# Attention's value matmuls over four token tiles at a time instead of two, in a hybrid encoder layer on one Trainium2 core

## The chip, the cores and the metric

The kernel runs on one NeuronCore of a Trainium2 chip. The metric is the device time of one execution in microseconds (us): the median of several runs. The engines are PE (TensorE; its weight loads are shown apart, as PEld), DVE (VectorE), ACT (ScalarE), POOL (GpSimd) and SP, which issues most DMAs.

## What is computed

One layer: a half-step feed-forward network, a mixer, a second feed-forward network, a final norm. The mixer has two groups of heads side by side, latent attention and retention, and one output projection over both. The change lies in attention alone, which has 8 heads of width 64 over 1024 tokens and no mask:

```python
def block(args):
    qn, qp = args
    s = (jnp.einsum('bqhd,bkhd->bhqk', qn, k_nope).astype(jnp.float32)
         + jnp.einsum('bqhr,bkr->bhqk', qp, k_pe).astype(jnp.float32))
    p = jax.nn.softmax(s * MLA_SCALE, axis=-1)
    return jnp.einsum('bhqk,bkhd->bqhd', p.astype(v.dtype), v)
```

## The kernel before, in words

All matmuls are in float32r. To keep float32's accuracy an operand is split in two by `split` (line 71): ACT casts the source to the upper part (line 75), DVE subtracts that from the source for the lower part (line 79). A product of two split operands is three matmuls (`mm3`, lines 115 to 120).

`attention` (line 1440) walks over 64 steps, 8 heads by 8 tiles of 128 queries. I count the tiles through all heads, 0 to 63. For one tile:

- `scores` (line 1481): six matmuls of 512 columns into a PSUM tile `mm` of 128 x 1024, of which there are two. DVE finds the row's extreme (`mx`, line 1490), ACT takes the exponential into `pr` (line 1494; two buffers) and its row sums.
- `flip` (line 1498): eight PE transposes (line 1507) turn `pr` over, four into each of two PSUM tiles `tp`; ACT's cast and DVE's subtraction bring them as split halves into `pT`, which holds two query tiles, 256 columns, and has two buffers.
- `values` (line 1513), once for two tiles: for each of 8 key tiles and each half of the split one matmul (line 1520), the values as weights and 256 columns of `pT` streaming, 16 in all into one PSUM tile `dn`. ACT copies the result out (`ota`, line 1523).
- `finish` (line 1526): two PE transposes (line 1530) back to token rows, a DVE reduction that adds the two halves (line 1532), a reciprocal of the sums (line 1535) and POOL's multiplication by it into `mixed` (line 1536), which is the queries' memory `qn`, free by then.

`queries` (line 1467) prepares a head's queries by eight transposes (line 1474); `keys` and `keys2` prepare the keys of two heads. The loop at the end gives the order in which steps are handed on: scores of step i, flip of i-1, values of i-2 and finish of i-4:

```python
            if 0 <= i - 1 < len(seq):
                flip(*seq[i - 1])
            for lag, fn in ((2, values), (4, finish)):
                if 0 <= i - lag < len(seq) and seq[i - lag][1] % 2 == 1:
                    fn(seq[i - lag][0], seq[i - lag][1] // 2)
```

A scheduler then lays the instructions of each engine out in a fixed order before the run; so an engine's instructions can stand between others than the code suggests, but on the chip each engine keeps its order, and waits by semaphores. After attention the generator `out_project` (line 1563) goes on with the output projection, whose first transposes (line 1602) and weights already stand among the last tiles.

Of the kernel before, what the change touches and what calls it, by code (L numbers as in the profile page):

```python
# [12 lines left out]
F32 = mybir.dt.float32  # L13
F32R = mybir.dt.float32r
# [3 lines left out]
ALU = mybir.AluOpType  # L18
# [3 lines left out]
P = 128  # L22
S = 1024
NT = S // P
# [4 lines left out]
HA, HR, HD = 8, 8, 64  # L29
# [32 lines left out]
class Layer:  # L62
# [1377 lines left out]
    def attention(self, small, pool, after):  # L1440
# [35 lines left out]
                hs = slice(half * 512, (half + 1) * 512)  # L1476
                self.split(ps[0:QH], qT[0:QH, 0, hs], qT[0:QH, 1, hs])

        sums, pts = {}, {}

        def scores(h, t):
            kT, qT = self.kT[h % 2], qTs[h]
            ts_ = slice(t * P, (t + 1) * P)
            ps = self.ps.tile([P, S], F32, name="mm")
            for n in range(2):
                ns = slice(n * 512, (n + 1) * 512)
                self.mm3(ps[:, ns], (qT[0:QH, 0, ts_], qT[0:QH, 1, ts_]),
                         (kT[0:QH, 0, ns], kT[0:QH, 1, ns]), True, True)
            mx = small.tile([P, 1], F32, name="mx", bufs=4)
            v.tensor_reduce(out=mx, in_=ps, axis=AX.X, op=ALU.min)  # L1490
            pr = pool.tile([P, S], F32, name="pr")
            if t % 2 == 0:
                sums[h, t // 2] = small.tile([P, 2], F32, name="sum", bufs=6)
            nc.scalar.activation(out=pr, in_=ps, func=AF.Exp, scale=-1.0, bias=mx,
                                 accum_out=sums[h, t // 2][:, t % 2:t % 2 + 1])
            pts[h, t] = pr

        def flip(h, t):
            pr = pts.pop((h, t))
            if t % 2 == 0:  # L1500
                pts[h, "T", t // 2] = pool.tile([P, 2, NT, 2 * P], F32R, name="pT")
            pT = pts[h, "T", t // 2]
            for half in range(2):
                ps = self.ps.tile([P, 512], F32, name="tp")
                for j in range(4):
                    kt = half * 4 + j
                    nc.tensor.transpose(ps[:, j * P:(j + 1) * P], pr[:, kt * P:(kt + 1) * P],  # L1507
                                        self.ident)
                k4, qs = slice(half * 4, half * 4 + 4), slice(t % 2 * P, (t % 2 + 1) * P)
                self.split(ps.rearrange("p (j q) -> p j q", j=4), pT[:, 0, k4, qs],  # L1510
                           pT[:, 1, k4, qs])

        def values(h, u):
            pT = pts.pop((h, "T", u))
            ps = self.ps.tile([P, 512], F32, name="dn")
            o = ps[:, 0:2 * P]
            for kt in range(NT):
                vl = self.vhl[:, kt, h].rearrange("p s d -> p (s d)")
                for x in range(2):
                    nc.tensor.matmul(o, vl, pT[:, x, kt], start=(kt == 0 and x == 0),  # L1520
                                     stop=(kt == NT - 1 and x == 1))
            ot = small.tile([P, 2 * P], F32, name="ota")
            nc.scalar.copy(out=ot, in_=o)
            pts[h, "O", u] = ot

        def finish(h, u):
            ot = pts.pop((h, "O", u))
            ps = self.ps.tile([P, 512], F32, name="dn")
            for j in range(2):
                nc.tensor.transpose(ps[:, j * P:(j + 1) * P], ot[:, j * P:(j + 1) * P], self.ident)  # L1530
            on = small.tile([P, 2, HD], F32, name="ona", bufs=1)
            v.tensor_reduce(out=on, in_=ps[:, 0:2 * P].rearrange("p (j s e) -> p j e s", j=2, s=2),
                            axis=AX.X, op=ALU.add)
            ri = small.tile([P, 2], F32, name="ri", bufs=6)
            v.reciprocal(out=ri, in_=sums.pop((h, u)))
            nc.gpsimd.tensor_tensor(out=mixed[:, 2 * u:2 * u + 2, h // 2, h % 2 * HD:(h % 2 + 1) * HD], in0=on,
                                    in1=ri.unsqueeze(2).broadcast_to([P, 2, HD]), op=ALU.mult)

        seq = [(h, t) for h in range(HA) for t in range(NT)]
        for i in range(len(seq) + 6):  # L1540
            if i < len(seq):
                h, t = seq[i]
                if t == 0 and h == 0:
                    queries(0, (0,))
                    keys(0)
                    queries(0, (1,))
                scores(h, t)
                if t == 1 and h + 1 < HA:
                    queries(h + 1)
                if t == 3:  # L1550
                    if h % 2 == 0:
                        keys2(h // 2)
                    elif h + 1 < HA:
                        keys(h // 2 + 1)
            if 0 <= i - 1 < len(seq):
                flip(*seq[i - 1])
            for lag, fn in ((2, values), (4, finish)):
                if 0 <= i - lag < len(seq) and seq[i - lag][1] % 2 == 1:
                    fn(seq[i - lag][0], seq[i - lag][1] // 2)
            if i - len(seq) in (-6, -5, -4, -3, 0):  # L1560
                next(after)

# [127 lines left out]
```

## Time and profile before

| | us |
|---|---|
| median of 3 runs | 2043.13 |
| lowest, highest | 2036.83, 2044.27 |
| the profiled execution | 2037.01 |
| its span, first to last instruction | 2035.3 |

| engine | busy us | share of the span |
|---|---|---|
| PE | 1974.2 | 97% |
| PE weight loads | 1697.3 | 83% |
| DVE | 1312.0 | 64% |
| ACT | 816.0 | 40% |
| POOL | 689.4 | 34% |

The numbers of the profile come from one execution; the profiled execution's own time is its span and some 1.7 us around it. Times in views count from the span's start. A matmul's row shows its pipelined length, longer than the distance to the next matmul's start; what a matmul takes from PE's queue is that distance. "idle before <-" says how long an engine stood and which instruction ended it. Attention lies between 1035 and 1270 us.

### The profile page before, as it was taken

The page shows a single profiled execution, that of the slowest core. Times are in us where ns is not written, and L with a number is a line of the kernel's source. Part 1 is how long each engine was busy: PE and PEld are TensorE (multiplying, and loading weights), DVE is VectorE, ACT ScalarE, POOL GpSimd, SP SyncE. Part 2 cuts the span into 40 slices and gives each one's busy share as a digit, 9 for nine tenths or more (in the row PEclk, how much of TensorE's full clock was granted, in tenths as well). Part 3 has the DMA queues.
Part 4 walks back from the last instruction along what each step waited for, and adds up shares of the span by engine and source line. Part 5 has one row for each costly group of instructions (what it writes and reads, how often), then busy time and mean ns, then how long its engine had stood idle before and what let it go on. Part 6 is the DMA issues. An engine that isn't in the chain of part 4 may idle for free.

```text
span 2035.3 us, 28607 instructions
## 1 busy us (share of the span) xinstructions
PE 1974.2 (97%) x10776; PEld 1697.3 (83%) x10776; DVE 1312.0 (64%) x2032; ACT 816.0 (40%) x1422; POOL 689.4 (34%) x614
## 2 busy tenths in 40 slices
PE   6999999999999999999999999999999999999998
PEld 4778888877778899998788888997788888878876
DVE  7766566676656545427878887448565665666566
ACT  5322222233444322236567776234223223234444
POOL 0256656673310013213521110000465665672012
PEclk9999999999999999999999999999999999999999
DMA  5244453468766011200100000141354444478773
GB/s 176 61 162 134 171 175 132 173 199 273 264 217 207 28 53 43 53 22 1 58 1 1 1 1 22 42 156 48 104 176 166 152 158 166 154 254 317 227 228 113
DMA packets 209338, 258.86 MB, mean 127 GB/s; under 512 B 14128, under 2 KB 126000, under 8 KB 209200
## 3 DMA queue, kind: packets, MB, share of 16 engines
q1 hardware_dynamic: 208048, 254.93, 37.8%
q8 instruction: 85, 1.39, 0.3%
q10 hardware_dynamic: 1152, 2.10, 0.3%
q14 instruction: 53, 0.43, 0.1%
HBM read 185.15 MB, written 71.83 MB: 126 GB/s over the span
## 4 chain that ended last, share of the span: by engine, by line
PE 40%; DVE 3%; DMA 3%; ACT 2%; issue 1%; POOL 1%; SPq 0%; ACTq 0%; DVEq 0%; POOLq 0%
PE mm L290 11%; PE dn L290 6%; PE dn L1520 3%; PE tp L290 3%; PE tp L1507 3%; PE mm L624 2%; DMA rawd<-wdt 2%; PE dn L118 2%; PE dn L120 2%; PE dn L119 2%; PE mm L118 1%; PE mm L120 1%; PE mm L119 1%; DVE wd L79 1%; PE dn L624 1%; PE tp L624 1%
## 5 line engine op out<-in xcount | busy, mean ns | idle before, releaser
L290 PE MATMUL mm<-xt,gu 128*128 128x512 f32 x1584 | 382.8, 390 | 0.4 <-ACT xt L75 0.3
L290 PEld LDWEIGHTS mm<-xt,gu 128*128 128x128 f32 x1584 | 296.5, 188 | 62.4 <-issue 1.0
L79 DVE TENSOR_TENSOR wd<-rawd,wd 128x1024 fp32r<-128x1024 f32 x143 | 194.9, 1368 | 126.1 <-ACT wd L75 125.9
L79 DVE TENSOR_TENSOR gu<-s,gu 128x512 fp32r<-128x512 f32 x176 | 180.8, 1028 | 139.6 <-ACT gu L75 139.6
L290 PE MATMUL dn<-x,gu 128*128 128x512 f32 x1056 | 258.8, 393 | 1.3 <-ACT x L75 1.3
L290 PEld LDWEIGHTS dn<-x,gu 128*128 128x128 f32 x1056 | 197.7, 189 | 42.8 <-ACT x L75 2.0
L75 ACT CAST wd<-rawd 128x1024 fp32r<-128x1024 f32 x143 | 150.2, 1052 | 193.0 <-DMA rawd<-wdt 59.6
L270 POOL TENSOR_TENSOR s<-raw 128x512 f32<-128x512 f32 x40 | 55.4, 1386 | 396.6 <-DMA raw<-in_ffn_w_up 198.2
L624 PE MATMUL mm<-wd 128*128 128x512 f32 x792 | 182.6, 390 | 2.1 <-DVE wd L79 2.1
L624 PEld LDWEIGHTS mm<-wd 128*128 128x128 f32 x792 | 148.1, 188 | 35.7 <-DVE wd L79 4.4
L79 DVE TENSOR_TENSOR gu<-raw,gu 128x512 fp32r<-128x512 f32 x132 | 123.1, 933 | 69.7 <-ACT gu L75 69.6
L322 DVE TENSOR_TENSOR h<-mm,h 128x512 f32<-128x512 f32 x176 | 120.8, 686 | 70.7 <-PE mm L290 70.3
L352 ACT ACTIVATE h<-h 128x512 f32<-128x512 f32 x44 | 27.8, 632 | 291.4 <-DVE h L322 291.4
L624 PE MATMUL dn<-wd 128*128 128x512 f32 x462 | 133.3, 392 | 8.5 <-DVE wd L79 8.5
L290 PE MATMUL tp<-xt,gu 128*128 128x512 f32 x528 | 128.0, 390 | 4.8 <-ACT gu L75 2.5
L624 PE MATMUL tp<-wd 128*128 128x512 f32 x462 | 130.2, 389 | 0.0
L75 ACT CAST gu<-s 128x512 fp32r<-128x512 f32 x176 | 104.2, 618 | 63.7 <-POOL s L271 59.6
L290 PE MATMUL mm<-x,gu 128*128 128x512 f32 x528 | 127.1, 390 | 0.0
L290 PEld LDWEIGHTS tp<-xt,gu 128*128 128x128 f32 x528 | 98.6, 188 | 27.3 <-ACT gu L75 3.4
L290 PEld LDWEIGHTS mm<-x,gu 128*128 128x128 f32 x528 | 99.0, 188 | 21.1 <-DVE h L322 0.6
L624 PEld LDWEIGHTS dn<-wd 128*128 128x128 f32 x462 | 85.8, 188 | 30.7 <-DVE wd L79 13.3
L633 POOL TENSOR_TENSOR h<-h,u 128x512 f32<-128x512 f32 x24 | 45.0, 1907 | 177.7 <-DMA rawd<-hid 89.2
(356 smaller groups left out, 3917.3 us busy)
## 6 DMA issues: line engine op xcount, KB each, us to landing
hid<-h SPq DMA_DIRECT2D x154, 256.0 KB, 3.2
rawd<-hid SPq DMA_DIRECT2D x154, 256.0 KB, 3.2
raw<-in_ffn_w_gate SPq DMA_DIRECT2D x52, 512.0 KB, 3.9
raw<-in_ffn_w_up SPq DMA_DIRECT2D x44, 512.0 KB, 4.1
rawd<-wdt SPq DMA_DIRECT2D x88, 256.0 KB, 3.7
early<-in_ffn_w_down SPq DMA_DIRECT2D x40, 512.0 KB, 5.6
wdt<-early SPq DMA_DIRECT2D x80, 256.0 KB, 4.5
rawd<-in_ffn_w_down SPq DMA_DIRECT2D x66, 256.0 KB, 3.4
```

Source lines behind the costliest of these rows:

```text
L75: a = nc.scalar.copy(out=hi, in_=src)
L79: b = eng.tensor_tensor(out=lo, in0=src, in1=hi.bitcast(F32), op=ALU.subtract)
L118: mm(out, l[0], r[0], start=start, stop=False)
L119: mm(out, l[0], r[1], start=False, stop=False)
L120: mm(out, l[1], r[0], start=False, stop=stop)
L270: tt(out=s[1], in0=u[:, h1], in1=u[:, h2], op=ALU.add)
L290: nc.tensor.matmul(out, l[:, p], r[:, q], start=start and dt == 0 and i == 0, stop=dt == 3 and i == 2, skip_group_check=True)
L322: v.tensor_tensor(out=out, in0=ps, in1=other, op=ALU.add)
L624: nc.tensor.matmul(out, w[:, p, 0, ts_], w[:, q, 1], start=start and i == 0, stop=stop and i == 2, skip_group_check=True)
L633: nc.gpsimd.tensor_tensor(out=q, in0=q, in1=u[:, t], op=ALU.add)
L1507: nc.tensor.transpose(ps[:, j * P:(j + 1) * P], pr[:, kt * P:(kt + 1) * P], self.ident)
L1520: nc.tensor.matmul(o, vl, pT[:, x, kt], start=(kt == 0 and x == 0), stop=(kt == NT - 1 and x == 1))
```

## The change

Values and finish now work on four tiles. `G = 4` takes the place of the 2 in the sums, in `values` and in `finish`, so that a value matmul has 512 columns and there are 8 x 2 blocks of 16. `pT` becomes two tiles, `pT0` and `pT1`, each with the four key tiles of one half, both parts of the split and 512 query columns. Each has one buffer, 32 KB a partition together, as the two buffers of `pT` before. A group's first flip can write `pT0` once the values of the group before have read it; so values and finish are handed on before the flip of the same step. `ota` has one buffer of 512 columns, the reduction writes straight into `mixed`, and POOL multiplies there in place.

```diff
-        sums, pts = {}, {}
+        sums, pts, G = {}, {}, 4
...
-            if t % 2 == 0:
-                pts[h, "T", t // 2] = pool.tile([P, 2, NT, 2 * P], F32R, name="pT")
-            pT = pts[h, "T", t // 2]
+            if t % G == 0:
+                pts[h, "T", t // G] = [pool.tile([P, 2, NT // 2, G * P], F32R, name=f"pT{half}",
+                                                 bufs=1) for half in range(2)]
...
-                k4, qs = slice(half * 4, half * 4 + 4), slice(t % 2 * P, (t % 2 + 1) * P)
-                self.split(ps.rearrange("p (j q) -> p j q", j=4), pT[:, 0, k4, qs],
-                           pT[:, 1, k4, qs])
+                pT, qs = pts[h, "T", t // G][half], slice(t % G * P, (t % G + 1) * P)
+                self.split(ps.rearrange("p (j q) -> p j q", j=4), pT[:, 0, :, qs], pT[:, 1, :, qs])
...
-            ps = self.ps.tile([P, 512], F32, name="dn")
-            o = ps[:, 0:2 * P]
+            o = self.ps.tile([P, 512], F32, name="dn")
...
-                    nc.tensor.matmul(o, vl, pT[:, x, kt], start=(kt == 0 and x == 0),
+                    nc.tensor.matmul(o, vl, pT[kt // 4][:, x, kt % 4], start=(kt == 0 and x == 0),
                                      stop=(kt == NT - 1 and x == 1))
-            ot = small.tile([P, 2 * P], F32, name="ota")
+            ot = small.tile([P, G * P], F32, name="ota", bufs=1)
...
-            for j in range(2):
+            for j in range(G):
                 nc.tensor.transpose(ps[:, j * P:(j + 1) * P], ot[:, j * P:(j + 1) * P], self.ident)
-            on = small.tile([P, 2, HD], F32, name="ona", bufs=1)
-            v.tensor_reduce(out=on, in_=ps[:, 0:2 * P].rearrange("p (j s e) -> p j e s", j=2, s=2),
+            on = mixed[:, G * u:G * (u + 1), h // 2, h % 2 * HD:(h % 2 + 1) * HD]
+            v.tensor_reduce(out=on, in_=ps.rearrange("p (j s e) -> p j e s", j=G, s=2),
                             axis=AX.X, op=ALU.add)
...
+            for lag, fn in ((2, values), (4, finish)):
+                if 0 <= i - lag < len(seq) and seq[i - lag][1] % G == G - 1:
+                    fn(seq[i - lag][0], seq[i - lag][1] // G)
             if 0 <= i - 1 < len(seq):
                 flip(*seq[i - 1])
-            for lag, fn in ((2, values), (4, finish)):
-                if 0 <= i - lag < len(seq) and seq[i - lag][1] % 2 == 1:
-                    fn(seq[i - lag][0], seq[i - lag][1] // 2)
```

How the scheduler laid it out. On PE before, in head 0 around the flip of tile 6 (L1507 is a flip's transposes, L1520 the values, L1530 the finish, L118 to L120 the scores):

```order
L1520 MATMUL dn<-pT,vhl 128x256 x4
L1507 MATMUL tp<-ident,pr 128x128 x8
L1520 MATMUL dn<-pT,vhl 128x256 x12
L1530 MATMUL dn<-ident,ota 128x128 x2
L118 MATMUL mm<-kT_8929,qTa 128x512
```

Values stand on both sides of the flip. On PE after, at the end of the first group of four, with the flips of tiles 4 and 5 (now L1509) and the scores between:

```order
L1520 MATMUL dn<-pT_9276,vhl 128x512 x8
L1520 MATMUL dn<-pT_9277,vhl 128x512 x8
L1509 MATMUL tp<-ident,pr 128x128 x8
L118 MATMUL mm<-kT_8929,qTa 128x512
L119 MATMUL mm<-kT_8929,qTa 128x512
L120 MATMUL mm<-kT_8929,qTa 128x512
L118 MATMUL mm<-kT_8929,qTa 128x512
L119 MATMUL mm<-kT_8929,qTa 128x512
L120 MATMUL mm<-kT_8929,qTa 128x512
L1509 MATMUL tp<-ident,pr 128x128 x8
```

All sixteen values stand in a row, and only scores stand between flips of a group. On ACT before, in head 2 (a pair of casts is one flip, ACTIVATE pr the exponential):

```order
L1523 COPY ota<-dn 128x256
L75 CAST pT<-tp 128x4x128 x2
L1494 ACTIVATE pr,sum<-mm,mx 128x1024
L75 CAST pT<-tp 128x4x128 x2
L1494 ACTIVATE pr,sum<-mm,mx 128x1024
L1523 COPY ota<-dn 128x256
```

On ACT after, in head 2 for the group of tiles 20 to 23:

```order
L1523 COPY ota<-dn 128x512
L75 CAST pT_9975<-tp 128x4x128
L75 CAST pT_9976<-tp 128x4x128
L75 CAST pT_9975<-tp 128x4x128
L75 CAST pT_9976<-tp 128x4x128
L1496 ACTIVATE pr,sum<-mm,mx 128x1024
L75 CAST pT_9975<-tp 128x4x128
L75 CAST pT_9976<-tp 128x4x128
L1496 ACTIVATE pr,sum<-mm,mx 128x1024
L75 CAST pT_9975<-tp 128x4x128
L75 CAST pT_9976<-tp 128x4x128
L1496 ACTIVATE pr,sum<-mm,mx 128x1024
```

The casts of the group's first two flips come one behind the other, then exponentials (now L1496) and casts by turns. Over all 64 flips, 27 now stand in two halves with scores or values between them, 10 before.

## Rows read from the trace of the kernel before

**Rows 1.** The page, part 1: busy time, share and instructions of each engine

```profile
PE 1974.2 (97%) x10776; PEld 1697.3 (83%) x10776; DVE 1312.0 (64%) x2032; ACT 816.0 (40%) x1422; POOL 689.4 (34%) x614
```

**Rows 2.** View of windows, attention: PE, PEld, DVE, ACT, POOL busy; clock; DMA

```profile
1100.00:1160.00 60.00, 59.86 (x407) 53.37 (x406) 49.01 (x74) 43.46 (x86) 6.12 (x11) 1.00 0.00 1
```

**Rows 3.** Grouped lines, attention 1035 to 1270 us: busy, mean ns, idle before

```profile
L79 DVE TENSOR_TENSOR pT<-tp,pT 128x512 fp32r<-128x512 f32 x128 | 83.1, 684 | 14.9 <-ACT pT L75 14.9
L1490 DVE TENSOR_REDUCE mx<-mm 128x1 f32<-128x1024 f32 x64 | 78.0, 1220 | 18.2 <-PE mm L120 18.2
```

**Rows 4.** Timeline of PE, four tiles of head 2: start, length, line

```profile
1101.25 1.04 PE L1507 MATMUL tp<-ident,pr 128*128 128x128 f32 x8
1102.05 0.48 PE L118 MATMUL mm<-kT,qTa 96*128 96x512 f32 x1
1102.37 0.39 PE L119 MATMUL mm<-kT,qTa 96*128 96x512 f32 x1
...
1103.50 0.64 PE L1520 MATMUL dn<-pT,vhl 128*128 128x256 f32 x4
1104.12 1.09 PE L1507 MATMUL tp<-ident,pr 128*128 128x128 f32 x8
1104.97 1.69 PE L1520 MATMUL dn<-pT,vhl 128*128 128x256 f32 x12
1106.49 0.38 PE L1530 MATMUL dn<-ident,ota 128*128 128x128 f32 x2
1106.63 0.48 PE L118 MATMUL mm<-kT,qTa 96*128 96x512 f32 x1
...
1108.11 1.04 PE L1507 MATMUL tp<-ident,pr 128*128 128x128 f32 x8
...
1114.95 1.04 PE L1507 MATMUL tp<-ident,pr 128*128 128x128 f32 x8
```

**Rows 5.** Timeline of ACT and PE's weight loads, the same stretch

```profile
1101.89 1.07 ACT L75 CAST pT<-tp 128x512 fp32r<-128x512 f32 x2 [1.53 <-PE tp L1507]
...
1102.85 1.13 ACT L1494 ACTIVATE pr<-mm,mx 128x1024 f32<-128x1024 f32 x1
...
1104.12 0.86 PEld L1507 LDWEIGHTS tp<-ident,pr 128*128 128x128 f32 x8 [0.18 <-ACT pr L1494]
...
1104.82 1.08 ACT L75 CAST pT<-tp 128x512 fp32r<-128x512 f32 x2 [0.75 <-PE tp L1507]
```

**Rows 6.** Grouped lines, retention stage 905 to 1010 us

```profile
L1197 DVE TENSOR_REDUCE rq<-tp 128x256 f32<-128x512 f32 x16 | 10.9, 681 | 0.0
```

**Rows 7.** Timeline of PE, the first tiles of attention

```profile
1043.69 1.46 PE L1507 MATMUL tp<-ident,pr 128*128 128x128 f32 x8
...
1046.14 0.88 PE L1520 MATMUL dn<-pT,vhl 128*128 128x256 f32 x6
1046.98 1.09 PE L1507 MATMUL tp<-ident,pr 128*128 128x128 f32 x8
...
1053.38 1.09 PE L1507 MATMUL tp<-ident,pr 128*128 128x128 f32 x8
```

**Rows 8.** Timeline of ACT, the same place

```profile
1045.71 1.13 ACT L1494 ACTIVATE pr<-mm,mx 128x1024 f32<-128x1024 f32 x1
```

**Rows 9.** Timeline of PE, the last group: first flip of four

```profile
1253.72 1.09 PE L1507 MATMUL tp<-ident,pr 128*128 128x128 f32 x8
```

**Rows 10.** Timeline of PE, where the output projection begins

```profile
1269.57 0.36 PE L118 MATMUL dn<-ckvT,kT 128*128 128x256 f32 x1
```

**Rows 11.** View of windows: a wait, the stretch behind it, two others

```profile
915.00:920.00 5.00, 2.47 (x21) 2.26 (x19) 3.73 (x5) 3.01 (x6) 1.31 (x2) 1.00 0.00 0
920.00:925.00 5.00, 4.12 (x23) 4.15 (x24) 4.49 (x8) 4.93 (x12) 0.00 (x0) 0.67 0.00 0
1000.00:1030.00 30.00, 27.49 (x158) 23.57 (x159) 27.94 (x65) 16.68 (x30) 16.67 (x23) 1.00 0.16 54
1040.00:1046.00 6.00, 6.00 (x28) 5.10 (x29) 3.31 (x6) 3.22 (x7) 0.30 (x1) 0.72 0.01 3
```

More of the change, by code (lines that the diff above doesn't have):

```diff
@@ L1491, in scores @@
             pr = pool.tile([P, S], F32, name="pr")
-            if t % 2 == 0:
-                sums[h, t // 2] = small.tile([P, 2], F32, name="sum", bufs=6)
+            if t % G == 0:
+                sums[h, t // G] = small.tile([P, G], F32, name="sum", bufs=6)
             nc.scalar.activation(out=pr, in_=ps, func=AF.Exp, scale=-1.0, bias=mx,
-                                 accum_out=sums[h, t // 2][:, t % 2:t % 2 + 1])
+                                 accum_out=sums[h, t // G][:, t % G:t % G + 1])
             pts[h, t] = pr
@@ L1499, in flip @@
             pr = pts.pop((h, t))
-            if t % 2 == 0:
-                pts[h, "T", t // 2] = pool.tile([P, 2, NT, 2 * P], F32R, name="pT")
-            pT = pts[h, "T", t // 2]
+            if t % G == 0:
+                pts[h, "T", t // G] = [pool.tile([P, 2, NT // 2, G * P], F32R, name=f"pT{half}",
+                                                 bufs=1) for half in range(2)]
             for half in range(2):
@@ L1528, in finish @@
             ps = self.ps.tile([P, 512], F32, name="dn")
-            for j in range(2):
+            for j in range(G):
                 nc.tensor.transpose(ps[:, j * P:(j + 1) * P], ot[:, j * P:(j + 1) * P], self.ident)
-            on = small.tile([P, 2, HD], F32, name="ona", bufs=1)
-            v.tensor_reduce(out=on, in_=ps[:, 0:2 * P].rearrange("p (j s e) -> p j e s", j=2, s=2),
+            on = mixed[:, G * u:G * (u + 1), h // 2, h % 2 * HD:(h % 2 + 1) * HD]
+            v.tensor_reduce(out=on, in_=ps.rearrange("p (j s e) -> p j e s", j=G, s=2),
                             axis=AX.X, op=ALU.add)
-            ri = small.tile([P, 2], F32, name="ri", bufs=6)
+            ri = small.tile([P, G], F32, name="ri", bufs=6)
             v.reciprocal(out=ri, in_=sums.pop((h, u)))
-            nc.gpsimd.tensor_tensor(out=mixed[:, 2 * u:2 * u + 2, h // 2, h % 2 * HD:(h % 2 + 1) * HD], in0=on,
-                                    in1=ri.unsqueeze(2).broadcast_to([P, 2, HD]), op=ALU.mult)
+            nc.gpsimd.tensor_tensor(out=on, in0=on,
+                                    in1=ri.unsqueeze(2).broadcast_to([P, G, HD]), op=ALU.mult)
         seq = [(h, t) for h in range(HA) for t in range(NT)]
```

## The prediction

> **What bounds the kernel now.** I read the page's busy shares first, then the windows of the attention stage, then the timelines of PE and ACT over four tiles. PE is busy for 97% of the span [rows 1], and in 60 us of attention for 59.86 us at a granted clock of 1.00, while DVE works 49.01 and ACT 43.46 of them [rows 2]. So in this stage the end is set by PE's queue, and a change is worth what it takes off that queue, less any wait it opens. The timeline shows the queue's pattern [rows 4]. Over two tiles stand one flip (the eight transposes of L1507), the scores of a tile, four value matmuls, the second flip, twelve value matmuls, two transposes of the finished outputs, and the scores of another tile. That runs from 1101.25 to 1108.11, 6.86 us; two such pairs end at 1114.95, so four tiles take 13.70 us.
>
> The reader should see one thing more there. From the flip at 1101.25 to the next at 1104.12 are 2.87 us, and the last part of it is a wait: PE's weight load idles 0.18 us until ACT has the exponentials [rows 5]. The chain is closed on ACT. A flip's cast starts 0.64 us after the flip (1101.25 to 1101.89), the pair of casts occupies ACT 0.96 us (to 1102.85), then the exponential of the next tile runs, and the next flip starts 1.27 us after it began (1104.12): 0.64 + 0.96 + 1.27 = 2.87 [rows 4, 5]. I call this the link. In the other half of a pair the flip-to-flip distance is 3.99 us (1104.12 to 1108.11), and the link is hidden under the twelve value matmuls. The kernel before runs so near to PE's limit because value matmuls stand in every second step.
>
> **The change, part by part.** *Width.* 512 value matmuls of 256 columns become 256 of 512. Twelve of the narrow ones take 1.52 us (1104.97 to 1106.49), which holds one switch from transposes to matmuls. That switch is seen at 1102.05: the first score matmul takes 0.32 us and the other five 1.13 us together, 0.23 each, so a switch costs 0.09 [rows 4]. A narrow matmul is then (1.52 - 0.09) / 12 = 0.12 us and a wide one 0.23: a block of four tiles costs 16 x 0.23 = 3.68 in place of 32 x 0.12 = 3.84. The width itself saves 0.16 us in four tiles, 2.6 us in all sixteen blocks. The Trainium skill, "TensorE: Matmul & The Clock Gate", section "Back-to-back issue gap", gives for a real stream a sustained pace of about 131 ns for 512 columns and 81 ns for 128. By that, with 98 ns for 256 columns in between, a pair of narrow matmuls costs 64 ns more than a wide one, and 256 pairs an estimated 16 us; the score matmuls here run at 0.23 us, so the trace does not agree and decides.
>
> *PE's work in four tiles after.* One flip takes 0.80 us (1101.25 to 1102.05) and the scores with their switch 1.45 (to 1103.50), together 2.25 [rows 4]. Four of those, the wide values and four output transposes at 0.07 (two take 0.14, 1106.49 to 1106.63) make 9.00 + 3.68 + 0.28 = 12.96 us: 0.74 less than 13.70, of which 0.28 are the two 0.14 us that the pair waits today.
>
> *The waits that come instead.* The values now stand in one block after four flips, so three of four steps have nothing on PE but a flip and scores, 2.25 us, against a link of 2.87. The changed order has ACT casting tile 1 of the group, then the exponential of tile 2, its casts, the exponential of tile 3. Tile 1's exponential was finished under the values of the group before, so the first step costs 2.25; the next two are links, 2.87 each; the last step is 2.25 and the values 3.68. From a group's first flip to the next: 2.25 + 2.87 + 2.87 + 2.25 + 3.68 = 13.92 us; the output transposes hide in the second link. That is 0.22 longer than 13.70, and over the fourteen groups between the fifth flip and the sixty-first, 3.1 us.
>
> *DVE in those steps.* A step asks DVE for two splits at 684 ns and one maximum at 1220 [rows 3], 2.59 us as it is shown, less than a link, so it is not the bound. The output's reduction becomes 16 of 512 columns in place of 32 of 256; retention has that form at 681 ns [rows 6]. It, the copy of the outputs on ACT and POOL's multiplication have no waiting reader before the next block or the output projection: cost nothing while the block lasts 3.68 us; if this cover went, some 0.7 us a group, 11 us.
>
> *One place for the transposed probabilities.* The cast of a group's first flip must wait until the values have left the first half. In the new order of PE all sixteen values stand ahead of that flip, and the cast comes 0.64 us after it, so the place is free: nothing, unless the flip were early. The overlap of the two halves that the change allows is not used by PE's order.
>
> *The half flips.* The new order breaks 27 of the 64 flips into two halves with score matmuls between, the old one 10. Each break adds one switch: 17 x 0.09 = 1.5 us.
>
> *The start.* There value matmuls covered two waits. Before: flip 1 at 1043.69, values from 1046.14, flip 2 at 1046.98, flip 4 at 1053.38 [rows 7]. The exponential of tile 2 begins at 1045.71 [rows 8], so flip 2 cannot leave before 1046.98 after either, and PE stands from 1046.14. From there one link to flip 3 (1049.85), 2.25 of flip and scores (1052.10), 3.68 of values: flip 4 at 1055.8, 2.4 us later. As the old kernel has by flip 4 left the same share of values behind as at flip 60, this difference is carried to the end.
>
> *The end.* Before, flip 60 to the first matmul of the output projection takes 1269.57 - 1253.72 = 15.85 us [rows 9, 10]. After: flip 61 at 2.25, flip 62 at 5.12, flip 63 at 7.99; its cast is done 1.2 us later; then sixteen values, sixteen transposes for the projection and the last finish. With the split that frees the transposes' buffer, I come to about 15.7. Taken as 0. SP's queue and everything outside attention stand in the same order.
>
> *Sum.* +2.4 + 3.1 + 1.5 + 0 = +7.0 us. The profiled execution took 2037.01 us (span 2035.3) and the median is 2043.13, so the former gives 2044.0 and I forecast **2050** for the median. The three runs lie 7.4 us apart; 0.5% (10.2 us) is about what a measurement of this kernel can tell from no change.
>
> *What no row shows.* Whether the link holds with this new order of ACT, between nothing (PE's work alone, 12.96) and three links in each group instead of two (+0.62). I take two, by the row at 1104.12, and keep both ends for the range.
>
> **The rivals.** *PE's work alone.* If the scores that run ahead into the second buffer cover the links, a group takes 12.96: fourteen groups give 14 x -0.74 = -10.4, and the start without its two waits (0.84 and 0.62) +1.0, the end 0, the breaks +1.5: -7.9, or 2035. For it speaks that the order was laid out with scores moved ahead and flips halved; against it that each flip needs an exponential that ACT issues behind the casts of the flip before.
>
> *A third link, slower.* If the exponential of a group's second tile falls behind the casts of its first, as where the order puts it so in the groups with half flips, the first step is a link too: +0.62 in each of fourteen groups, +8.7, that is 2043.1 + 7.0 + 8.7 = 2059. It decides where PE reaches the second flip of a group before that exponential is 1.27 us old. Against it: the 3.68 us of values leave ACT time to finish it in most groups.
>
> *The clock falls.* After a wait the granted clock did fall to the lower level here: in 915 to 920 PE was busy for 2.47 of 5 us and the next 5 us had 0.67; 1040 to 1046 had 0.72 behind the idle stretch ahead of the first flip [rows 11]. At levels of 1 and 0.5, 0.72 over 6 us is 3.4 us at half speed, 1.7 us lost. Once in each group would be 14 x 1.7 = 24 us more, 2074. Against it: 1000 to 1030 was busy for 27.49 of 30 us and kept 1.00 [rows 11]; the groups after would idle 0.96 of 13.92 us, a like share in shorter pieces. The Trainium skill, in the same page's section "A second HAM failure mode: psum-queue depth-cycling", warns that frequent short idles between groups of matmuls make the clock go up and down; the rows named here, with idles of this kind, do not show that.
>
> **How the numbers follow.** My forecast 0.66 (its own range 2044 to 2055), PE's work alone 0.16, a third link 0.13, the clock 0.05. The range is 2035 to 2060: from the second case to the third; it leaves out the clock and the outer tails. Slower by over 0.5% (above 2053.3) are the third link, the clock and 0.04 of the forecast: 0.22. Faster by over 0.5% (below 2032.9) is only the tail of PE's work alone, 0.03. Within: 0.75.
>
> **What would show it.** In PE's timeline after: 2.87 us between the second, third and fourth flip of a group and about 13.9 from group to group; waits of transposes on ACT's pr of 0.6 us, two in a group, some 30 and 18 us in all; value matmuls 0.23 apart; flip 4 some 2.4 us later than before; clock 1.00 after the first 6 us. Wrong: if those waits stay under 5 us, if ACT or DVE shows no idle in the stage, or if times outside attention move.

## The result and the profile after

The changed kernel takes 2055.98 us (median of 4 runs, 2053.59 to 2060.44), the kernel before in the runs beside it 2040.66 (2036.83 to 2044.27, 4 runs): 1.0072 times as long, 95% interval 1.0056 to 1.0089. The forecast was 2050 us, its own range 2044 to 2055, the whole range 2035 to 2060. So the time is at the upper end, and slower by over 0.5%, a case that had 0.22, while "within 0.5%" had 0.75.

The page of the kernel after, part 1, answers to [rows 1]:

```profile
PE 1981.8 (97%) x10520; PEld 1683.1 (82%) x10520; DVE 1305.5 (64%) x2000; ACT 817.2 (40%) x1406; POOL 685.0 (33%) x598
```

PE has 256 matmuls fewer and DVE 32 instructions fewer, yet PE is busy 7.6 us longer. The view of windows of the kernel after (PE, PEld, DVE, ACT, POOL busy, then the clock) shows the same 60 us as [rows 2], and the first stretch as in [rows 11]:

```profile
1040.00:1046.00 6.00, 4.43 (x19) 3.70 (x20) 3.85 (x5) 3.56 (x7) 1.91 (x2) 0.74 0.01 3
1060.00:1100.00 40.00, 38.57 (x217) 30.98 (x215) 31.60 (x44) 29.51 (x55) 4.37 (x5) 1.00 0.00 1
1100.00:1160.00 60.00, 58.13 (x325) 46.40 (x324) 44.76 (x62) 42.41 (x78) 4.97 (x6) 1.00 0.00 1
```

PE now stands for 1.87 of 60 us, where it stood for 0.14. The clock stays at its upper level. The view of waits, attention from 1035 to 1290 us, says what they are for (total, times, longest); "ACT pr" is the exponential:

```profile
DVE pT L79 <- ACT pT L75: 53.7, 31, 3.6
...
PEld tp L1509 <- ACT pr L1496: 12.4, 15, 2.2
PE tp L1509 <- ACT pr L1496: 7.4, 12, 1.8
```

DVE's line was 14.9 us [rows 3], and PE's transposes waited 2.0 for the exponential before (same view). The forecast had some 30 such waits and 18 us of them. PE's transposes have 12 and 7.4 us, their weight loads 15 and 12.4 us; the two overlap, so the sum of 19.8 us isn't time that PE lost.

From PE's timelines the attention stage falls into three parts. I count from flip to flip, as the prediction did; "after" is the output projection's first matmul.

| | before | after | difference | forecast |
|---|---|---|---|---|
| flip 0 to flip 4 | 13.41 | 15.89 | +2.48 | +2.4 |
| flip 4 to flip 60 | 200.34 | 209.71 | +9.37 | +4.6 |
| flip 60 to the projection | 15.85 | 16.03 | +0.18 | 0 |

That is +12.03 us in the stage. The span of the profiled execution grew by 16.5; the other 4.5 lie outside the stage (1.6 before flip 0, 2.9 behind it). Behind the projection's first matmul the profiled kernels of this study, whose work there is all but the same, took from 762.8 to 769.7 us, so I count those 4.5 as scatter. Part of it is the clock: in the change's profile the view of windows has 0.83 from 1380 to 1390 us and from 1473 to 1483, where before's has 1.00; by the working of the prediction that is up to 1.7 us each. So it is the middle part that has to be explained: 4.8 us more than forecast.

A group without queries and keys in it shows the forecast's pattern. Timeline of PE, kernel after, flips 56 to 60:

```profile
1253.16 1.03 PE L1509 MATMUL tp<-ident,pr 128*128 128x128 f32 x8
...
1255.40 1.07 PE L1509 MATMUL tp<-ident,pr 128*128 128x128 f32 x8
...
1258.27 1.09 PE L1509 MATMUL tp<-ident,pr 128*128 128x128 f32 x8
...
1261.20 1.09 PE L1509 MATMUL tp<-ident,pr 128*128 128x128 f32 x8 [0.44 <-ACT pr L1496]
...
1263.51 3.82 PE L1520 MATMUL dn<-pT,vhl 128*128 128x512 f32 x16
1267.17 1.04 PE L1509 MATMUL tp<-ident,pr 128*128 128x128 f32 x8
```

The steps are 2.24, 2.87, 2.93, and 5.97 with the values: 14.01 us, forecast 13.92. The third flip comes one link after the second, the fourth waits 0.44 us for its exponential.

### The profile page after: what moved, and what is told of

It is laid out like the page before. It is cut to its first block, busy times and chain, and to the rows that moved or that the text cites. A ratio compares the mean times of both kernels' runs of the same rounds, so it can differ in the third digit from the quotient of the medians.

```text
span 2051.8 us, 27992 instructions
## 1 busy us (share of the span) xinstructions
PE 1981.8 (97%) x10520; PEld 1683.1 (82%) x10520; DVE 1305.5 (64%) x2000; ACT 817.2 (40%) x1406; POOL 685.0 (33%) x598
## 4 chain that ended last, share of the span: by engine, by line
PE 37%; DVE 4%; ACT 4%; DMA 3%; issue 1%; POOL 1%; SPq 0%; ACTq 0%; DVEq 0%; POOLq 0%
PE mm L290 10%; PE dn L290 6%; PE dn L1520 3%; PE tp L290 3%; PE tp L1509 2%; DMA rawd<-wdt 2%; PE mm L624 2%; PE dn L119 2%; PE dn L118 2%; PE dn L120 2%; DVE wd L79 1%; PE mm L118 1%; PE dn L624 1%; PE tp L624 1%; ACT pr L1496 1%
## 5 line engine op out<-in xcount | busy, mean ns | idle before, releaser
L79 DVE TENSOR_TENSOR pT<-tp,pT 128x512 fp32r<-128x512 f32 x128 | 83.2, 684 | 53.9 <-ACT pT L75 53.7
```

What stands on the lines that cost most here:

```text
L79: b = eng.tensor_tensor(out=lo, in0=src, in1=hi.bitcast(F32), op=ALU.subtract)
```

## The experiments

In the table, "plain" is four tiles without queries and keys (half of flip 52 to 60); "sixteen" is flip 20 to flip 36, which holds two heads' queries and one pair's keys; "extra" is sixteen less four times plain, the price of queries and keys. Sixteen tiles hold 96 score matmuls in every run. Single groups of four tiles can't be compared so, since the scheduler moves scores between them: 24 would be four tiles' worth, but in the change the groups with keys (the first from flip 8 to 12) hold 30 and those from flip 16, 32 and 48 hold 19. Ratios are to the kernel before as it ran beside each run.

| run | flip 4 to 60 | plain | sixteen | extra | median us, ratio (95%) |
|---|---|---|---|---|---|
| before | 200.34 | 13.71 | 57.58 | 2.74 | 2040.66 |
| the change | 209.71 | 14.05 | 60.58 | 4.40 | 2055.98, 1.0072 (1.0056 to 1.0089) |
| four_narrow | 206.00 | 14.13 | 58.94 | 2.44 | 2046.21, 1.0030 (1.0014 to 1.0046) |
| two_swap | 198.78 | 13.65 | 57.06 | 2.48 | 2038.50, 0.9984 (0.9969 to 1.0000) |
| lag2_four | 210.50 | 13.47 | 60.61 | 6.73 | 2052.05, 1.0057 (1.0040 to 1.0073) |
| lag2_manual | 297.09 | | | | 2152.59, 1.0547 (1.0512 to 1.0581) |
| four_keys5 | 207.14 | 14.04 | 59.28 | 3.12 | 2049.01, 1.0044 (1.0031 to 1.0056) |
| two_oneplace | 205.74 | 13.79 | 58.85 | 3.71 | 2044.89, 1.0019 (1.0008 to 1.0029) |
| lag2_two | 200.80 | 13.39 | 57.99 | 4.45 | 2037.26, 0.9991 (0.9979 to 1.0003) |
| four_split | 212.01 | 14.28 | 60.97 | 3.87 | 2056.61, 1.0082 (1.0069 to 1.0096) |

The first theory was the prediction's: three of four flips have no values beside them, so the link from exponential to flip is uncovered.

**Is it the width?** Each wide matmul as two narrow ones:

```diff
-                    nc.tensor.matmul(o, vl, pT[kt // 4][:, x, kt % 4], ...)
+                    for c in range(2):
+                        cs = slice(c * 2 * P, (c + 1) * 2 * P)
+                        nc.tensor.matmul(o[:, cs], vl, pT[kt // 4][:, x, kt % 4, cs], ...)
```

> The changed kernel, but each value matmul of 512 columns is two of 256 (256 more matmuls, the same columns). By the price of the prediction (0.12 us a narrow matmul, 0.23 a wide one) a block costs 3.84 us in place of 3.68: 16 x 0.16 = +2.6 us on the changed kernel, whose stretch from the flip of tile 4 to that of tile 60 was 209.7 us: about 212, a median of some 2058 to 2059. If the width of a matmul were worth much (64 ns a pair, the estimate by the Trainium skill's page on TensorE), it would be +16 us: 225 in the stretch, 2072. If the values' columns lie under waits anyway: +0.

It came out faster than the change, by 3.7 us from flip 4 to 60, though it issues twice as many value matmuls. The price of the width itself is as forecast. Sixteen wide matmuls take 3.66 us (1263.51 to 1267.17 in the timeline above). Timeline of PE, this run, flips 58 to 60:

```profile
1257.68 0.28 PE L1522 MATMUL dn<-pT,vhl 128*128 128x256 f32 x1
1258.28 1.09 PE L1509 MATMUL tp<-ident,pr 128*128 128x128 f32 x8 [0.31 <-ACT pr L1496]
...
1260.61 3.87 PE L1522 MATMUL dn<-pT,vhl 128*128 128x256 f32 x31
1264.32 1.04 PE L1509 MATMUL tp<-ident,pr 128*128 128x128 f32 x8
```

Here 31 narrow ones take 3.71 us, 0.12 each, so 32 would take 3.83, 0.17 more than the wide ones. One of the 32 stands ahead of the fourth flip, under its wait for the exponential, and so a plain group is only 0.08 us slower (14.13 against 14.05). The gain is in "extra", 2.44 against 4.40. For a block of 32 instructions the scheduler had laid scores, values and keys out otherwise. So the width is worth 0.17 us a group, and the layout around queries and keys 2 us in sixteen tiles. Over the stretch the run stands 5.66 us above before, and 14 times the plain groups' 0.42 is 5.9: in this layout queries and keys cost no more than before.

**Is it the order of steps, or the single place?** The kernel before with values and finish handed on ahead of the flip, then the same with one buffer:

```diff
+            for lag, fn in ((2, values), (4, finish)): ...
             if 0 <= i - 1 < len(seq):
                 flip(*seq[i - 1])
-            for lag, fn in ((2, values), (4, finish)): ...
```

```diff
-                pts[h, "T", t // 2] = pool.tile([P, 2, NT, 2 * P], F32R, name="pT")
+                pts[h, "T", t // 2] = pool.tile([P, 2, NT, 2 * P], F32R, name="pT", bufs=1)
```

> The kernel before, with only the order of steps changed as in the changed kernel: values and finish are handed on ahead of the flip of the same step; groups of two, two buffers of pT as before. Theory one, the group of four leaves three of four flips without values beside them and so uncovers the wait of a flip for ACT's exponential: here values still stand in every second step, so the stretch from the flip of tile 4 to that of tile 60 stays within 4 us of the 200.3 of before, the median within 0.3% of it. Rival, the order of steps is what costs, since all values of a pair now stand in one piece: the stretch takes most of the +9.4 us of the changed kernel, 206 or more.

> The run with groups of two and values ahead of the flip, with one buffer for the transposed probabilities in place of two. If the single place costs nothing, as the prediction took it (all values of a pair stand ahead of the flip that writes it again, and the cast comes 0.6 us behind that flip): within 2 us of the 198.8 from the flip of tile 4 to that of tile 60, or faster or slower only by the order. If it costs a wait of a cast for the last value matmul: 28 pairs at 0.2 to 0.6 us, 204 to 215.

The order alone costs nothing; it is 1.6 us shorter than before. The single place, however, added 7.0 us to it (205.74 against 198.78), which the prediction had at nothing. Plain groups hardly move (13.65 to 13.79); "extra" goes from 2.48 to 3.71, and one group stood out of the row with 18.39 us. The buffer also made the scheduler lay these groups out anew. In the view of waits, 1055 to 1262 us, no cast waits for the values, which would be the wait for the place itself; ACT's copy of the outputs waits 15.4 us for them, and PE's weight loads for values wait 3.9 us for DVE's split, where the run with two buffers has none and 1.3. So the price sits in the order that one buffer led to. Two places of 512 columns weren't tried.

**Does the link bind?** Flips two steps behind their scores, with a third buffer for exponentials:

```diff
-            pr = pool.tile([P, S], F32, name="pr")
+            pr = pool.tile([P, S], F32, name="pr", bufs=3)
...
-            for lag, fn in ((2, values), (4, finish)):
+            for lag, fn in ((3, values), (5, finish)):
...
-            if 0 <= i - 1 < len(seq):
-                flip(*seq[i - 1])
+            if 0 <= i - 2 < len(seq):
+                flip(*seq[i - 2])
```

> The changed kernel with the flip of a tile two steps behind its scores instead of one, values and finish a step later too, and three buffers for the exponentials; the room for them comes from the keys' temporary, which now lies in the output weights' buffers, so the first fetch of those weights starts later (step 52). Theory one, the flip's wait for the exponential is the cost: the exponential is done a step before its flip, the link of 2.87 us is open, a group comes down towards PE's own 12.96 us, and the stretch from the flip of tile 4 to that of tile 60 towards 14 x 12.96 + 10 = 191 us, 18 less than the changed kernel; if DVE (2.59 us a step as shown) binds the three steps without values instead, a group is 3 x 2.59 + 5.93 = 13.7 and the stretch about 202. Waits of the flip's transposes and weight loads on the exponential, 19.8 us in the changed kernel, fall below 5. Rival, the single place of the transposed probabilities or the half flips set the pace: the stretch stays at 206 or more.

> As the run with flips two steps behind, but with attention's instructions in the order of the code on every engine in place of the scheduler's: no flip stands in two halves, exponentials and casts alternate on ACT. Theory one with the scheduler's order as a second cost: 191 to 202 us from the flip of tile 4 to that of tile 60, some 2 to 5 us less than with the scheduler's order. If the scheduler's half flips cost nothing beyond a switch each (0.09 us): within 2 us of that run. If the order of the code leaves queries and keys on the path: slower than that run.

> The kernel before with the flip two steps behind its scores, three buffers for exponentials and the keys' temporary in the output weights' buffers. If the link to the exponential is what is left of waiting at two tiles, PE's own work remains: 14 x 13.12 + 11 for queries and keys = 195 us from the flip of tile 4 to that of tile 60, 5 less than before, and a median some 4 us below before's. If the link only moves to the scores' buffers, as in the run with four tiles: 200 or more and no gain.

The link opened, and the stretch stayed (210.50). The view of waits of this run, 1050 to 1290 us:

```profile
DVE pT L79 <- ACT pT L75: 52.4, 31, 3.5
...
PEld mm L118 <- ACT pr L1496: 12.0, 17, 1.8
PEld tp L1509 <- DVE pT L79: 7.5, 21, 1.0
PE mm L118 <- ACT pr L1496: 6.5, 13, 1.4
```

No row of flips waiting for the exponential is left, but now the scores wait for it, since it frees their buffer. The 13.47 us of a plain group, where I had expected 12.96 to 13.7, are no sure gain: from flip 52 to 60 this run holds 42 score matmuls where the change has 47 and most runs 48, since its scores had run ahead. At 0.23 us each the six missing from 48 are 1.4 us, so a full plain group would take an estimated 14.2, and "extra" would be some 4 us in place of 6.73. At two tiles, with all 48, plain groups did fall, from 13.71 to 13.39, but "extra" rose to 4.45 and nothing was gained, as the second of the two cases expected there had it. So opening the link moved the wait to another buffer, and the stretch kept its length.

The second run adds one line around the loop, which keeps the code's order on every engine:

```diff
+        with tc.manual_schedule():
             for i in range(len(seq) + 7): ...
```

Everything is far slower: ACT takes each exponential ahead of the casts of an older flip. The run's waits, 1050 to 1370 us:

```profile
ACT pr L1496 <- DVE mx L1492: 130.0, 61, 3.3
DVE pT L79 <- ACT pT L75: 122.8, 67, 4.2
...
PEld tp L1509 <- DVE pT L79: 44.9, 43, 2.9
PE tp L1509 <- DVE pT L79: 33.6, 20, 2.6
```

The exponential waits for the maximum, the casts stand behind it, the split behind the casts, the next flip behind the split. I had expected 191 to 202 us and a gain from whole flips; it measured 297.09, and of the three cases set down the time fits only the last, "slower than that run". ACT's order is worth far more here than unbroken flips. A part of it is the clock, though. View of windows, flip 4 to flip 60 of this run:

```profile
1067.15:1364.24 297.09, 231.37 (x1131) 181.86 (x1130) 160.43 (x218) 148.82 (x272) 16.05 (x20) 0.89 0.02 8
```

The same 1131 matmuls keep PE busy for 231.37 us, and for 202.99 in the scheduler's order, where the clock stayed at 1.00: 28.4 us more at a mean granted clock of 0.89. The other 58.2 us are idle time of PE, 65.72 against 7.51.

**What do queries and keys have to do with it?** Both kernels with head 0's queries and keys for all heads (the other heads' query transposes, key matmuls and their splits are left out):

```diff
-            kT, qT = self.kT[h % 2], qTs[h]
+            kT, qT = self.kT[0], qTs[0]
...
-                if t == 1 and h + 1 < HA:
-                    queries(h + 1)
-                if t == 3: ...
```

> The changed kernel with the queries and keys of head 0 used for all eight heads; the other heads' query transposes, key matmuls and their splits are left out, so every group is the plain one and hardly any flip stands in two halves. To be read beside the kernel before with the same cut. Theory one, the plain group was forecast right (two links, 13.92 us) and the rest of the loss arises where queries, keys and half flips meet the links: flip 4 to flip 60 takes 14 x 13.9 to 14.0 = 195 to 196 us, 3 to 5 more than the other. Rival, the block of values costs in every group alike: the distance to the other stays at 9.

> The kernel before with the queries and keys of head 0 used for all eight heads, the same work left out. Bound by PE, four tiles take between 13.12 (flips, scores, values and output transposes alone) and 13.70 us (the plain group of before): 184 to 192 us from flip 4 to flip 60.

View of windows, flip 4 to flip 60, first the four-tile kernel with the cut (196.29 us, PE busy 190.21), then the two-tile kernel (191.71, all of it busy):

```profile
1053.74:1250.03 196.29, 190.21 (x1066) 156.19 (x1065) 142.70 (x196) 130.30 (x238) 8.57 (x14) 1.00 0.00 1
```

```profile
1053.69:1245.40 191.71, 191.71 (x1289) 170.96 (x1288) 149.44 (x225) 129.35 (x252) 11.15 (x28) 1.00 0.00 1
```

One execution each, they take 2041.14 and 2034.32 us. Every group is alike now, 14.00 to 14.05 and 13.69 to 13.70 us, and the distance is 4.58 instead of 9.37. So half of the loss is the plain group, 14 x 0.33, as the prediction described it; the other 4.79 us come with queries and keys, and with the half flips that go with them.

**Is DVE the bound beside the link?** After the lagged runs I held that the long block of values starves DVE, which then sets the pace (theory two). The same two kernels, with the row's extreme taken over half the columns and scores scaled down:

```diff
-            v.tensor_reduce(out=mx, in_=ps, axis=AX.X, op=ALU.min)
+            v.tensor_reduce(out=mx, in_=ps[:, 0:512], axis=AX.X, op=ALU.min)
```

> The same cut of the changed kernel, and DVE looks for a row's extreme in 512 of the 1024 columns only (0.6 us less of DVE a tile; the scores are scaled down so that exponentials stay finite). Theory two, which the runs with flips two steps behind suggest: the block of values leaves DVE without work for some 3.5 us a group, so that DVE's 10.2 us a group, pressed into the rest, set the pace beside the link: then a group falls by 0.6 to 1.0 us, to PE's 12.96 or a little over, 182 to 186 us from flip 4 to flip 60. Theory one alone, the link by ACT (flip, casts, exponential, flip), in which DVE's maximum has no part: no more than 0.2 us a group, 192 to 196.

> The same for the kernel before, as the control. PE is the bound there and DVE has room: between 0 and 0.3 us a group less than without the cut in the maximum, so within 4 us of it from flip 4 to flip 60.

The four-tile kernel fell to 190.40 us, its groups to 13.56 to 13.61 but for one of 13.87 (0.44 less), the control by 0.5 us in all, to 191.24. One execution each, they take 2032.53 and 2027.15 us. Windows of the four-tile kernel, flip 4 to flip 60:

```profile
1055.37:1245.77 190.40, 190.16 (x1066) 153.87 (x1065) 119.20 (x196) 129.34 (x238) 8.57 (x14) 1.00 0.00 1
```

PE's idle time went from 6.08 us to 0.24. The timeline of PE shows how, in one group:

```profile
1152.65 1.07 PE L1509 MATMUL tp<-ident,pr 128*128 128x128 f32 x8
...
1155.37 0.60 PE L1509 MATMUL tp<-ident,pr 128*128 128x128 f32 x4
1155.73 0.49 PE L118 MATMUL mm<-kT,qTa 96*128 96x512 f32 x1
1156.05 0.40 PE L119 MATMUL mm<-kT,qTa 96*128 96x512 f32 x1
1156.29 0.39 PE L120 MATMUL mm<-kT,qTa 96*128 96x512 f32 x1
1156.57 0.63 PE L1509 MATMUL tp<-ident,pr 128*128 128x128 f32 x4
...
1158.42 0.62 PE L1509 MATMUL tp<-ident,pr 128*128 128x128 f32 x4
```

The flips are still 2.72 and 3.05 us apart, so the links remain. But the score matmuls of the following tile now run inside them, and the group's last step falls from 5.97 to 5.57 us. Theory two said 182 to 186 us, the link alone 192 to 196; the measured 190.40 lies between. The shorter maximum and the layout that it led to came together, so the shares of the two stay open. What the pair shows is that PE need not stand in a link when scores run in it, here with 23.5 us less of DVE's work in the stretch (119.20 against 142.70). It also has 28 of the 56 flips of the stretch in two halves, the kernel with the whole maximum none, and PE hardly stands: half flips by themselves are no loss.

**Keys elsewhere.** In the changed kernel the keys are handed on at tile 3 of an odd head, a step without values. Moved to tile 5:

```diff
-                if t == 3:
-                    if h % 2 == 0:
-                        keys2(h // 2)
-                    elif h + 1 < HA:
-                        keys(h // 2 + 1)
+                if t == 3 and h % 2 == 0:
+                    keys2(h // 2)
+                if t == 5 and h % 2 and h + 1 < HA:
+                    keys(h // 2 + 1)
```

> The changed kernel with the keys of the next pair of heads handed on at tile 5 of an odd head instead of tile 3, which is the step whose values also stand there; nothing else is changed, and fewer flips stand in two halves. Theory: half of the loss (9.4 us less the 4.6 of the plain groups) arises because the keys' matmuls, casts and copies now fall into the stretch without values, where ACT and DVE already set the pace (key groups of 17.4 us, against 15.2 in the run with narrow matmuls, where the scheduler had laid them otherwise). Then the key groups lose about 2 us each, three of them, and the stretch from the flip of tile 4 to that of tile 60 takes 202 to 205 us in place of 209.7; the median falls by 5 to 8 us to some 2049. Rival, queries and keys cost this wherever they stand: 208 or more.

The median is the expected 2049, but not by the expected way: the stretch fell by 2.6 us to 207.14, where 202 to 205 was expected, and lies just short of the rival's bound of 208. Sixteen tiles with queries and keys fell by 1.3 (4.40 to 3.12 extra) in the first two of the three key groups; the third stood out with 21.2 us for its four tiles, which hold six score matmuls more than those of the others. The 17.4 and 15.2 us that the expectation compares hold 30 and 25 score matmuls, so their difference isn't the price of the keys. So the place of the keys is worth something, but not all of the 4.8 us.

**The block in two.** Eight values, half of the next flip and a score tile between, then eight values (`values` and `flip` take the half as an argument):

```diff
+            for lag, fn in ((2, lambda h, u: values(h, u, 0)), (3, lambda h, u: values(h, u, 1)),
+                            (5, finish)): ...
+            if 2 <= i < len(seq) + 2 and seq[i - 2][1] % G == 0:
+                flip(*seq[i - 2], (1,))
             if 0 <= i - 1 < len(seq):
-                flip(*seq[i - 1])
+                flip(*seq[i - 1], (0,) if seq[i - 1][1] % G == 0 else (0, 1))
```

> The changed kernel, with the block of sixteen values handed on in two parts: first the eight of the first half of the transposed probabilities, then the first half of the next group's flip, which may write that place now, the next scores, then the other eight values and the second half of the flip. Width, single place, queries and keys stay. Theory two, what costs is one block of 3.7 us in which DVE finds nothing to do, after which DVE and ACT are pressed: now a score tile and half a flip stand inside the block, DVE's idle time waiting for casts falls well below the changed kernel's 51.5 us, plain groups come from 14.0 down to 13.0 to 13.4 us, and the stretch from the flip of tile 4 to that of tile 60 takes 197 to 203 us; the median comes to before's, 2037 to 2045. Rival, the single place or the width costs by itself, or queries and keys do wherever they fall: the stretch stays at 206 or more. A new wait is possible: a value's matmul that waits for the split of the half flip just before it.

A clear miss: 212.01 us, plain groups 14.28. The view of waits of this run, 1050 to 1300 us:

```profile
DVE pT L79 <- ACT pT L75: 38.9, 26, 2.7
...
DVE mx L1492 <- PE mm L120: 13.8, 7, 2.1
PEld tp L1509 <- DVE pT L79: 12.3, 42, 1.3
PEld mm L118 <- ACT pr L1496: 10.3, 30, 1.5
```

DVE's wait for casts fell to 38.9 us (51.5 in the change, 1050 to 1290 us), but 13.8 us of waiting for scores took its place, and the half flips wait more for DVE's split. With this run theory two has no support as a way to get the time back.

## Why the prediction was right and wrong

**The bound and the plain group: right.** The steps of a plain group are 2.24, 2.87, 2.93 and 5.97 us where the forecast has 2.25, 2.87, 2.87 and 5.93. The term "+0.22 x 14 = +3.1" measured 0.33 x 14 = +4.6 with queries and keys cut out. That DVE is no bound beside the link held for the links' length; but with less of DVE's work scores ran ahead into them, so DVE had a part in what a link costs, which the prediction didn't see.

**The step that failed: "The half flips", with no term for queries and keys.** It priced 17 further breaks at a switch each, +1.5 us, and the sum has nothing for the work of queries and keys, which takes it to cost as much after as before. Before, PE is the bound, and two queries and a pair of keys cost 2.74 us in sixteen tiles. After, with the flips on a chain through ACT and DVE, they cost 4.40, and together with the half flips 4.8 us more over the stretch where the term said 1.5. (That the middle part was also 4.8 over its forecast is chance: 3.3 of it are from here, 1.5 from the plain groups.) The timeline of ACT in the kernel after, a group with keys, shows one way in:

```profile
1077.81 1.28 ACT L75 CAST kT<-dn 64x512 fp32r<-64x512 f32 x2 [0.36 <-PE dn L120]
1078.99 1.11 ACT L1496 ACTIVATE pr<-mm,mx 128x1024 f32<-128x1024 f32 x1
...
1080.22 1.07 ACT L1465 COPY k<-dn 64x512 f32<-64x512 f32 x2
1081.31 1.07 ACT L75 CAST pT<-tp 128x512 fp32r<-128x512 f32 x2
1082.27 1.13 ACT L1496 ACTIVATE pr<-mm,mx 128x1024 f32<-128x1024 f32 x1
```

The timeline of PE beside it:

```profile
1078.31 1.04 PE L1509 MATMUL tp<-ident,pr 128*128 128x128 f32 x8
1079.10 0.48 PE L118 MATMUL mm<-kT,qTa 96*128 96x512 f32 x1
...
1083.54 0.50 PE L118 MATMUL mm<-kT,qTa 96*128 96x512 f32 x1 [0.63 <-ACT pr L1496]
1083.88 0.60 PE L1509 MATMUL tp<-ident,pr 128*128 128x128 f32 x4
1084.23 0.48 PE L119 MATMUL mm<-kT,qTa 96*128 96x512 f32 x1
1084.56 0.60 PE L1509 MATMUL tp<-ident,pr 128*128 128x128 f32 x4
```

The cast of the flip at 1078.31 begins at 1081.31, 3.00 us later in place of 0.64 [rows 4, 5], behind the keys' casts, an exponential and two copies. The next exponential stands behind that cast, and PE's scores wait 0.63 us for the buffer that it frees. That such layouts and not the keys' own work cost the time is shown by the run with narrow matmuls and by the one with keys at tile 5, which got 2.0 and 1.3 us of "extra" back with all of that work in place.

The breaks themselves are nearly free. Four transposes take 0.35 us (1083.88 to 1084.23), eight take 0.79 (1078.31 to 1079.10), so two halves take 0.09 less than a whole flip, and that pays for the second first matmul behind transposes, 0.32 in place of 0.23.

PE's idle time alone doesn't show the 4.8 us. View of windows, flip 4 to flip 60, before and after:

```profile
1053.38:1253.72 200.34, 199.91 (x1355) 178.28 (x1354) 164.41 (x247) 148.13 (x286) 19.70 (x34) 1.00 0.02 6
1057.46:1267.17 209.71, 203.30 (x1132) 163.02 (x1131) 158.47 (x218) 149.52 (x272) 16.16 (x20) 1.00 0.02 6
```

PE is idle for 0.43 and 6.41 us, and without queries and keys for 0 and 6.08. But a matmul's pipelined length covers short waits, and the distances between starts don't. Most of PE's rows keep one pace: 0.11 us from transpose to transpose, 0.03 from the last of them to a matmul, 0.23 from a wide matmul to the next, 0.12 from a narrow one, and 0.32 or 0.20 from the first one behind transposes. Counted so, the stretch is 196.5 us of work before and 194.6 after, without queries and keys 187.0 and 184.8. The rest is waiting: 3.9 and 15.1 us, without queries and keys 4.7 and 11.5. The pace is an estimate from these rows, good to a microsecond or so in each sum, but the difference hardly depends on it: 4.4 of the 4.8 us are waits and 0.4 is work. With queries and keys in the changed kernel the flips wait less, 9.0 us in place of 12.1, but the scores wait 3.6, the values 1.6 and the finish 1.0 us, where without them none waits by more than 0.04 us. Which of keys, queries and half flips sets each of these waits isn't settled.

**"One place": not borne out.** It was set at nothing. At two tiles the single place cost 7.0 us, of which plain groups had 2.0 (14 x 0.14), the rest came with queries and keys. At four tiles no such price shows in the run with narrow matmuls, which has the single place too: there queries and keys cost no more than before.

**Width: right.** 0.16 us a block was forecast, 0.17 measured; at the pace above, PE's work in the stretch fell by 2.2 us without queries and keys (187.0 to 184.8), and 14 x 0.16 is 2.2. The estimate of 16 us after the Trainium skill, "TensorE: Matmul & The Clock Gate", section "Back-to-back issue gap", isn't borne out.

**Start and end: right.** +2.48 against +2.4, +0.18 against 0. Both profiles had the clock's lower level behind flip 0 (0.72 and 0.74 over 6 us), so the start is compared like with like.

**The rivals.** PE's work alone (12.96 us a group) didn't come; 13.56 to 13.61 with half of the maximum left out was the nearest for groups with all their scores. The third link came in no group from flip 4 on: their first steps take 2.05 to 2.27 us. Its 2059 us lies near the result all the same, and that is luck: the median stands inside the whole range because the range reaches up to that case. The clock of the change stayed at 1.00 from flip 4 to flip 60, with idles of up to 0.6 us. In the run in the code's order, where PE waited up to 3.0 us at a time, it went up and down, 0.89 on the mean. The Trainium skill's section "A second HAM failure mode: psum-queue depth-cycling" on the same page tells of a clock that goes up and down with short idles between groups of matmuls; the change doesn't show that with its idles, the run in the code's order does with its longer ones.

**The sum.** The stage's +12.0 on 2040.66 is 2052.7, where the forecast's +7.0 on 2043.13 gave 2050; the remaining 3.3 us to the median of 2055.98 is as large as the scatter outside the stage. By the medians the change costs 15.3 us, over twice the 7.0 of the forecast. The mechanism was named and its sign was right; two terms, +3.1 and +1.5, were too small by 1.5 and 3.3 us. They moved the result over the bound of 0.5%.

No run that does all of the work beats the kernel before by what can be told apart. The nearest is the exchanged order at two tiles, 0.9984 (0.9969 to 1.0000).

## What to carry to other kernels

When a change uncovers a chain between engines, price each kind of repetition by itself: work that was hidden in some of them (here queries and keys on ACT and DVE) joins the chain, and it cost as much as the plain repetition. A wait that is opened moves to the next buffer, so ask what holds that one: flips two steps behind were free of the exponential, and the scores then waited for it. And where a scheduler lays the instructions out, an edit worth a tenth or two of a microsecond a group can be worth less than the layout that it causes; compare plain groups with plain groups before the edit gets the credit, and count that both hold the same instructions.

## What the runs showed of the hardware

Two kernels with the same order of PE's instructions up to flip 4, the change and the one with keys at tile 5, took 15.89 and 14.37 us from flip 0 to flip 4. The windows of the second show the clock:

```profile
1040.00:1046.00 6.00, 5.32 (x34) 4.41 (x35) 4.50 (x6) 4.13 (x8) 0.29 (x1) 1.00 0.01 3
```

The granted clock is 1.00 there and 0.74 in the change's profile. The 1.5 us between them are then the cost of the lower level, near the 1.7 us that the prediction worked out for such a stretch. Both waited 1.78 us ahead of flip 0. The profile of before, with flip 0 at 1039.97 us, had 0.72 there [rows 11], the one with keys at tile 5, with flip 0 at 1039.95, has 1.00. So the fall came in some executions and not in others behind a like wait, and a term for it belongs into the range and not into the sum.
